# Moving a subtract from VectorE to GpSimd while a recurrence runs

## The chip, the cores and the metric

The kernel runs on one core of a Trainium2 chip. The metric is the device time of one execution in microseconds, the median of several runs. The engines of the core that matter here are TensorE (PE, matmuls), VectorE (DVE, elementwise work), ScalarE (ACT, activations and copies), GpSimd (POOL, here nearly idle) and the DMA queue that SyncE (SP) feeds.

## The reference

One layer of a decoder trunk, in float32, for a sequence of 1024 tokens and a width of 1024. Cut to what matters:

```python
h = rms_norm(x, norm_mix_pre)
proj = h @ w_in                                  # r, k, v, low ranks | S5 input | two gates
gates = jax.nn.sigmoid(proj[..., 2304:] + b_gate)
g_rwkv, g_s5 = jnp.split(gates, 2, axis=-1)
o_rwkv = rwkv7_branch(proj[..., :1792], ...) @ w_branch_rwkv     # a recurrence over the tokens
o_s5 = s5_branch(proj[..., 1792:2304], ...) @ w_branch_s5        # a diagonal state space model and a GLU (w_glu)
mixed = (g_rwkv * o_rwkv + g_s5 * o_s5) @ w_out
x = x + rms_norm(mixed, norm_mix_post)
h = rms_norm(x, norm_ffn_pre)
z = conv(h @ w_up)                               # causal, width 3
f = (gelu(gate) * val) @ w_down                  # gate, val: the halves of z
return x + rms_norm(f, norm_ffn_post)
```

The recurrence (RWKV-7) keeps a 64x64 state for each of 8 heads: `S = S * w + (S a) b' + v k'`, and each token reads `S r`.

## The kernel before, in words

**Matmuls in two parts.** Each operand of the large matmuls is split into a high part (rounded to the matmul's type, fp32r) and a low part (the float32 value less the high part). A product then takes three matmuls: high by high (L172), low activations by high weights (L173), high activations by low weights (L174). `mm3_steps` issues them for one 128x128 weight tile and 512 tokens; that is a step, and the kernel's planner counts 0.68 us for it.

**Weights.** `load_w` (L142) brings the weights in, 512 columns at a time: a DMA on SP's queue into a raw tile `wf` (L155), a cast by ScalarE into the high part `wh` (L156), and a subtract by VectorE into the low part `wl` (L157). There are 4 `wh` and 4 `wl` buffers; the raw tiles come from the pool `self.wp` (2 buffers) and, while `self.wfp` names a second pool, from that too (2 more). All of it is issued at the high priority HPW. L157 runs 171 times: for w_in, the low ranks, w_glu, w_br (the branch projections), w_out, and the first tiles of w_up.

**Stages.** `front_half` (L1816) runs the projections and the S5 branch, then, from L1850 on, the recurrence together with the rest of the mixing sub-layer. `build` goes on with the end of the mixing (`mix_out`), the up-projection (`fast_up`) and the down-projection (`down`).

**The recurrence.** The tokens come in two halves (th = 0, 1), each in 8 chunks of 64. For each half there is a preparation (`rwkv_front`), the inversion of triangular matrices (`rwkv_inv`: transposes at L784 and L798, then 30 pairs of short VectorE steps, L795 and L797, one after another, and copies at L773), a second level (`rwkv_level`: transposes at L812, matmuls at L822 and L832), the chain over 8 chunks (`rwkv_chain`: small matmuls, and U and S on VectorE at L890, L903, L904), and an output stage (`rwkv_out`). The matmuls of the projections, gates and merges are the filling between the small matmuls of these lanes.

**What sets the order.** The order on TensorE is written out by hand: `drive` (L185) takes a step of a lane when its due time has come by the planner's clock, and steps of the filling (`background`) otherwise. The order on the other engines is planned when the program is built, by priorities and estimated durations, and is fixed from then on; each engine works through its queue in order.

**The filling during the recurrence.** First the rest of the projections (r, k, v and gates, with their weights from w_in), then the merge of the first half of the tokens (`merge`): `gate` (L1198) multiplies a branch by its projection into a PSUM bank `gm` (2 banks in this stage) and VectorE empties the bank at L1203; `glu_tile` is the GLU of the S5 branch. Then follow the S5 branch's merge for the second half (`merge_s5`) and the output projection of the first half (`outproj(0, ...)`). When that is done `self.mark` is set and the stage ends (L1859).

**GpSimd's queue before.** In this stage it holds a few memsets (L624, L672), four small products (L627), the DMAs that export the bonus terms (L731, after VectorE's L730), and the DMAs that load late gates (L1195). At the very end of the kernel it does three adds (L1672).

Of the kernel before, what the change touches and what calls it, by code (L numbers as in the profile page):

```python
# [9 lines left out]
F32 = mybir.dt.float32  # L10
# [3 lines left out]
ALU = mybir.AluOpType  # L14
# [52 lines left out]
class Kern:  # L67
# [74 lines left out]
    def load_w(self, *srcs, pool=None):  # L142

        nc = self.nc
        wh, wl = [], []
        wp = pool or self.wp
        with self.tc.high_priority(HPW):
            for src in srcs:
                for o in range(0, src.shape[1], 512):
                    n = min(512, src.shape[1] - o)  # L150
                    h = wp.tile([128, 512], F32R, tag="wh", name=self.nm("wh"), bufs=4 if pool else NWH)
                    l = self.lx() if pool else wp.tile([128, 512], F32R, tag="wl", name=self.nm("wl"), bufs=NWL)
                    self.wfs = (self.wfs + 1) % (2 if self.wfp is None else 4)
                    f = (self.wp, self.wfp)[self.wfs // 2].tile([128, 512], F32, tag="wf", name=self.nm("wf"), bufs=NWF)
                    nc.sync.dma_start(f[:, :n], src[:, o:o + n])  # L155
                    nc.scalar.copy(h[:, :n], f[:, :n])  # L156
                    nc.vector.tensor_tensor(l[:, :n], f[:, :n], h[:, :n].bitcast(F32), ALU.subtract)  # L157
                    wh.append(h)
                    wl.append(l)
        return wh, wl  # L160
# [802 lines left out]
    def start(self, pool):  # L963
# [70 lines left out]
        for i in range(2):  # L1034
            for b in range(4):
                load_w(b, i)
            for k in range(4 * i, 4 * i + 4):
                if k:
                    load_x(0, k)
# [776 lines left out]
    def front_half(self):  # L1816

        tc = self.tc
        self.h = [None, None]
        self.now = self.credit = 0.0  # L1820
        self.wfs, self.wfp = 0, None
        self.fill_prio, self.acc = HPW, {}
        self.mark, self.chained = False, False
        self.s5_in_done, self.stored, self.mixed_in, self.all_in, self.open = -1, None, False, False, 0
        with tc.tile_pool(name="lxp", bufs=4) as self.lxp, tc.tile_pool(name="s5c", bufs=1) as self.s5c, \
                tc.tile_pool(name="u8p", bufs=1) as u8p, tc.tile_pool(name="eva", bufs=NEVA) as self.evp, \
                tc.tile_pool(name="psx", bufs=1, space=PSUM) as self.psx:
            self.ps, self.ngm = self.psx, 4
            self.u8 = [u8p.tile([128, 8, 128], F32, name=f"u8_{b}") for b in range(4)]
            with tc.tile_pool(name="xp", bufs=1) as xp:  # L1830
                with tc.high_priority(HPN):
                    self.setup(xp)
                    self.s5w = {}
                    self.start(xp)
                    self.setup_vecs()
                with tc.high_priority(HP):
                    self.s5_setup()
                self.fill = [self.mix_in()] + [self.gate_tiles(m) for m in range(14)] + [
                    self.merge_loads(), self.gate_tiles(14, 15)]
                self.outs, self.yr = 0, []  # L1840
            with tc.tile_pool(name="s5p", bufs=1) as self.s5p:
                self.s5d = [{} for _ in range(4)]
                self.tabs = self.s5_done = -1
                self.drive([(HP2, self.s5_lane()), (HP, self.tab_lane())])
                self.drain(lambda: self.mixed_in and not self.open)
        self.early_stack = ExitStack()
        self.rka = self.early_stack.enter_context(tc.tile_pool(name="rka", bufs=1, side="right"))
        with tc.tile_pool(name="evb", bufs=NEV) as self.evp, tc.tile_pool(name="rk", bufs=1) as self.rk, \
                tc.tile_pool(name="psy", bufs=1, space=PSUM) as self.psx:
            self.ps, self.ngm = self.psx, 2  # L1850
            self.rwkv_setup()
            self.wfp = self.rk
            self.ds = [[{}, {}], [{}, {}]]
            self.grams = 0
            self.fronts, self.masked, self.preps, self.chains, self.chunks, self.outs, self.z = 0, 0, 0, 0, 0, 0, {}
            self.pts = [self.tg("pt", 2, (128, 8, 4)) for th in range(2)]
            mg, self.mx0, self.first, self.ys5, self.xs5, self.brk, self.fac = [], [], [], [], [], [], []
            self.drive([(HP2, self.prep_lane(0)), (HP2, self.prep_lane(1)), (HP2, self.chain_lane()), (HP, self.out_lane(mg))])
            self.drain(lambda: self.mark)  # L1859
            self.wfp = None  # L1860

    def s5_lane(self):
        for b in range(4):
# [143 lines left out]
```

## Time and profile before

| | |
|---|---|
| median of 3 runs | 1463.06 us (1462.29 to 1465.25) |
| the profiled execution | 1461.26 us, its span 1459.5 us |
| granted TensorE clock, mean | 0.986 |
| busy: TensorE, VectorE, ScalarE, GpSimd | 1402.2, 1087.5, 746.7, 34.9 us |
| L157, all 171 | 117.2 us on VectorE, 688 ns each |
| L156, all 171 | 105.2 us on ScalarE, 618 ns each |

How to read the lines of a profile: a row of a group or of a timeline names the engine, the line of the kernel, the operation, the output and the inputs by the names of their tiles, the shape and type, and the count; in brackets or behind a bar stands the idle time of the engine just before, and what ended it (its releaser). L157 is line 157 of the kernel before. A row of a table by stretches gives for each stretch of the span the busy microseconds and, in brackets, the number of instructions of each engine, then the granted clock of TensorE (1.00 is full speed), the share of time that the DMA engines were busy, and GB/s. A row of waits reads: who waited, for whom, microseconds in total, how often, the longest.

### The profile page before, as it was taken

Reading aid. Unit: us, or ns where it says so; the run is one execution under the profiler, and the core shown is the slowest. Engines: PE = TensorE matmul, PEld = TensorE weight load, DVE = VectorE, ACT = ScalarE, POOL = GpSimd, SP = SyncE. Lnnn points to the kernel's source line nnn. Section 1 sums busy time; section 2 is a strip of 40 time slices with the busy share of each in tenths; the row PEclk is TensorE's granted clock in tenths of the full one; section 3 lists DMA queues with packets and bytes.
Section 4 is the critical chain, followed back from the end, with each engine's and each line's share of the span. In section 5 each row is a group of like instructions: output and inputs, shape, how many; then the busy total and the mean of one; then the engine's idle time right before and its main releaser. Section 6 shows DMA issues by size and latency. Waiting matters only on the chain. (4 is left out here: it accounts for less than half of the span.)

```text
span 1459.5 us, 23887 instructions
## 1 busy us (share of the span) xinstructions
PE 1402.2 (96%) x9156; PEld 1142.9 (78%) x9156; DVE 1087.5 (75%) x1783; ACT 746.7 (51%) x1197; POOL 34.9 (2%) x80
## 2 busy tenths in 40 slices
PE   7999999999999989899999999999999999999996
PEld 5778888878878767678788887888888887888785
DVE  8986886378327788548688898777777777597677
ACT  7667775453424564535455464454544445444451
POOL 0000000000000000000000000000000000000001
PEclk9999999999999999899999999999999999999998
DMA  7454433542413565433555543222222228934723
GB/s 221 116 190 128 144 117 108 188 146 80 139 60 110 162 193 165 138 111 116 172 195 180 158 133 122 87 83 76 75 84 87 87 73 273 328 112 144 239 79 115
DMA packets 119682, 202.04 MB, mean 138 GB/s; under 512 B 28672, under 2 KB 34944, under 8 KB 119568
## 3 DMA queue, kind: packets, MB, share of 16 engines
q1 hardware_dynamic: 113296, 182.43, 39.4%
q0 software_dynamic: 4544, 15.80, 2.9%
q10 hardware_dynamic: 1728, 2.29, 0.4%
q8 instruction: 72, 1.18, 0.3%
q14 instruction: 42, 0.34, 0.1%
HBM read 148.04 MB, written 50.33 MB: 136 GB/s over the span
## 5 line engine op out<-in xcount | busy, mean ns | idle before, releaser
L172 PE MATMUL gm<-hh,wh 128*128 128x512 f32 x672 | 276.2, 411 | 9.1 <-DVE hl L1203 4.6
L173 PE MATMUL gm<-hl,wh 128*128 128x512 f32 x672 | 264.8, 394 | 0.0
L174 PE MATMUL gm<-hh,wl 128*128 128x512 f32 x672 | 264.6, 394 | 0.0
L156 ACT CAST wh<-wf 128x512 fp32r<-128x512 f32 x171 | 105.2, 618 | 140.9 <-PE gm L173 72.5
L157 DVE TENSOR_TENSOR wl<-wf,wh 128x512 fp32r<-128x512 f32 x171 | 117.2, 688 | 76.2 <-ACT wh L156 75.6
L172 PEld LDWEIGHTS gm<-hh,wh 128*128 128x128 f32 x672 | 127.5, 190 | 41.5 <-DVE hl L1203 5.7
L174 PEld LDWEIGHTS gm<-hh,wl 128*128 128x128 f32 x672 | 127.7, 190 | 27.8
L173 PEld LDWEIGHTS gm<-hl,wh 128*128 128x128 f32 x672 | 127.8, 190 | 24.7 <-issue 1.0
L1626 PE MATMUL d<-xl,wh 128*128 128x512 f32 x308 | 120.7, 392 | 2.1 <-DVE xl L227 2.0
L1625 PE MATMUL d<-xh,wh 128*128 128x512 f32 x308 | 120.8, 392 | 2.1 <-ACT xh L226 2.1
L1627 PE MATMUL d<-xh,wl 128*128 128x512 f32 x308 | 120.6, 392 | 0.0
L1451 PE MATMUL rp<-t,h 128*128 128x512 f32 x216 | 84.4, 391 | 1.5 <-ACT p L1465 1.5
L1453 PE MATMUL rp<-t,l 128*128 128x512 f32 x216 | 84.2, 390 | 0.5 <-DVE l L227 0.5
L1452 PE MATMUL rp<-t,h 128*128 128x512 f32 x216 | 84.1, 389 | 0.0
L1626 PEld LDWEIGHTS d<-xl,wh 128*128 128x128 f32 x308 | 58.2, 189 | 15.5 <-DVE xl L227 3.4
L1625 PEld LDWEIGHTS d<-xh,wh 128*128 128x128 f32 x308 | 58.2, 189 | 14.6 <-ACT xh L226 2.4
L1627 PEld LDWEIGHTS d<-xh,wl 128*128 128x128 f32 x308 | 58.1, 189 | 12.0
L226 ACT CAST h<-r 128x1024 fp32r<-128x1024 f32 x34 | 35.8, 1054 | 61.1 <-PE rp L1452 29.6
L227 DVE TENSOR_TENSOR l<-r,h 128x1024 fp32r<-128x1024 f32 x34 | 41.6, 1225 | 29.2 <-ACT h L226 27.7
L1472 DVE SCALAR_TENSOR_TENSOR y<-zv,vecs,y 128x1023 f32<-128x1023 f32 (+1 forms) x36 | 46.1, 1281 | 8.5 <-ACT y L1470 8.5
L1465 ACT COPY p<-rp 128x512 f32<-128x512 f32 x54 | 31.0, 574 | 36.6 <-PE rp L1453 36.6
L1451 PEld LDWEIGHTS rp<-t,h 128*128 128x128 f32 x216 | 40.5, 188 | 11.1 <-ACT p L1465 2.4
(459 smaller groups left out, 3127.6 us busy)
## 6 DMA issues: line engine op xcount, KB each, us to landing
r<-in_w_up_dram SPq DMA_DIRECT2D x36, 512.0 KB, 3.6
wf<-in_w_in_dram SPq DMA_DIRECT2D x62, 256.0 KB, 3.0
st<-in_w_down_dram SPq DMA_DIRECT2D x55, 256.0 KB, 4.0
st<-ACT SPq DMA_DIRECT2D x44, 256.0 KB, 4.3
wf<-in_w_up_dram SPq DMA_DIRECT2D x36, 256.0 KB, 2.9
ACT<-y POOLq DMA_DIRECT2D x18, 512.0 KB, 2.9
GT<-ev SPq DMA_DIRECT2D x32, 256.0 KB, 2.5
wf<-in_w_br_dram SPq DMA_DIRECT2D x32, 256.0 KB, 2.6
```

Of the source, the lines that this page charges most:

```text
L156: nc.scalar.copy(h[:, :n], f[:, :n])
L157: nc.vector.tensor_tensor(l[:, :n], f[:, :n], h[:, :n].bitcast(F32), ALU.subtract)
L172: mm(ps, a, xh[k], start=k == 0, stop=False)
L173: mm(ps, a, xl[k], start=False, stop=False)
L174: mm(ps, b, xh[k], start=False, stop=k == n - 1)
L1451: mm(ps, wh[:, c], xh, start=first and k == 0, stop=False, skip_group_check=True)
L1452: mm(ps, wh[:, c], xl, start=False, stop=False, skip_group_check=True)
L1453: mm(ps, wl[:, c], xh, start=False, stop=k == 3, skip_group_check=True)
L1472: V.scalar_tensor_tensor(y[:, lag:], z[:, 0:1024 - lag], self.vec(nme, i), y[:, lag:], ALU.mult, ALU.add)
L1625: mm(ps, wh[:, c], xh[:, x], start=start, stop=False, skip_group_check=True)
L1626: mm(ps, wh[:, c], xl[:, x], start=False, stop=False, skip_group_check=True)
L1627: mm(ps, wl[:, c], xh[:, x], start=False, stop=stop, skip_group_check=True)
```

## The change

`load_w` takes the engine of the subtract from a new attribute, `self.weng`. It is VectorE at the start, GpSimd from the moment at which the recurrence's stage names its second pool for raw tiles, and VectorE again when that stage has ended. Nothing else is edited: the casts, the loads and TensorE's order stay as they are.

```diff
@@ load_w
                     nc.scalar.copy(h[:, :n], f[:, :n])
-                    nc.vector.tensor_tensor(l[:, :n], f[:, :n], h[:, :n].bitcast(F32), ALU.subtract)
+                    self.weng.tensor_tensor(l[:, :n], f[:, :n], h[:, :n].bitcast(F32), ALU.subtract)
@@ front_half, at its start
-        self.wfs, self.wfp = 0, None
+        self.wfs, self.wfp, self.weng = 0, None, self.nc.vector
@@ front_half, after rwkv_setup
-            self.wfp = self.rk
+            self.wfp, self.weng = self.rk, self.nc.gpsimd
@@ front_half, when the stage has ended
-            self.wfp = None
+            self.wfp, self.weng = None, self.nc.vector
```

In the program's order 33 of the 171 loads come before the switch, 78 while it is set (30 of w_in, 24 of w_br, 8 of w_glu, 16 of w_out), and 60 after it.

## The prediction

> **What bounds the kernel now.** I read the first two parts of the page first, then the table by stretches, then what TensorE waited for, and only then single rows.
>
> ```profile
> span 1459.5 us, 23887 instructions
> PE 1402.2 (96%) x9156; PEld 1142.9 (78%) x9156; DVE 1087.5 (75%) x1783; ACT 746.7 (51%) x1197; POOL 34.9 (2%) x80
> ```
>
> TensorE (PE) is busy for 96% of the span and GpSimd (POOL) for 2%. So a gain can only come out of the idle time of TensorE, or out of its clock, in the stage that the change touches. The table by stretches shows how much that is (columns: stretch, its length, busy us and count of PE, PEld, DVE, ACT, POOL, then granted clock, DMA share, GB/s; the sum runs over 250 to 712).
>
> ```profile
> 450.00:500.00 50.00, 47.69 (x350) 39.34 (x349) 44.43 (x90) 29.38 (x60) 1.08 (x2) 0.97 0.47 144
> 500.00:550.00 50.00, 43.53 (x297) 34.03 (x297) 41.00 (x85) 28.88 (x52) 1.08 (x2) 0.97 0.63 196
> 550.00:600.00 50.00, 41.13 (x325) 32.87 (x325) 42.26 (x80) 27.82 (x51) 0.00 (x0) 0.89 0.56 172
> 650.00:700.00 50.00, 50.00 (x410) 40.27 (x400) 37.73 (x75) 25.26 (x46) 2.13 (x4) 1.00 0.33 101
> sum 462.00, PE 440.03 PEld 350.11 DVE 296.13 ACT 219.54 POOL 8.80; mean PE 44.00 PEld 35.01 DVE 29.61 ACT 21.95 POOL 0.88
> ```
>
> Over the whole recurrence TensorE idles 462.0 - 440.0 = 22 us, and 15.3 us of that lie between 500 and 600 (6.5 + 8.9), where VectorE (DVE) is 82 to 85% busy. At 650 to 700 VectorE is 75% busy and TensorE loses nothing. The waits of TensorE in the same window name what came late:
>
> ```profile
> PE gm L172 <- DVE hl L1203: 4.6, 2, 3.9
> PE gm L172 <- DVE ev L1203: 3.1, 2, 2.2
> PE rp L822 <- DVE ld L812: 3.0, 1, 3.0
> PE cz L822 <- ACT hh L231: 2.2, 1, 2.2
> PE rp L756 <- DVE ld L730: 1.7, 1, 1.7
> ```
>
> No line names L157, the subtract that the change moves. TensorE waits for PSUM banks that the gating of the merges (L1203, on VectorE) has not yet emptied, and for small steps of the recurrence. So the subtract matters only as work that stands ahead of those steps in VectorE's queue.
>
> **The change part by part.** Which instructions move: the 33 loads before the switch keep VectorE, the 60 after it too, and 171 - 33 - 60 = 78 move. The windows of that line show them, the first row for the stretch of the second inversion, the second for all:
>
> ```profile
> L157 DVE TENSOR_TENSOR wl<-wf,wh x171: 644/689/737, 48.1 to 879.0; 128x512 fp32r<-128x512 f32 x171
> 523.00:569.00 46.00, 10.26 (x15) 0.96 0.58 182
> 273.00:700.00 427.00, 53.33 (x78) 0.98 0.42 134
> ```
>
> Removed from VectorE: 78 x 0.69 = 53.3 us of busy time. Added to POOL: the same instruction on GpSimd. The nearest rows are the three subtracts' cousins at the very end, of the same 128x512 size with two SBUF inputs, and the VectorE work beside them:
>
> ```profile
> L1672 POOL TENSOR_TENSOR r<-r,A x2: 1262/1472/1682, 1448.6 to 1449.9; 128x512 f32<-128x512 f32 x2
> L1672 DVE TENSOR_TENSOR r<-r,A x2: 679/699/719, 1449.7 to 1451.7; 128x512 f32<-128x512 f32 x2
> 1448.64 2.94 POOL L1672 TENSOR_TENSOR r<-r,A 128x512 f32<-128x512 f32 x2 [211.48 <-DVE r L1671]
> 1449.74 0.72 DVE L1672 TENSOR_TENSOR r<-r,A 128x512 f32<-128x512 f32 x1
> 1451.85 1.65 POOL L1672 TENSOR_TENSOR q<-q,A 128x512 f32<-128x512 f32 x1 [0.27 <-DVE q L1671]
> 1451.69 0.68 DVE L1672 TENSOR_TENSOR r<-r,A 128x512 f32<-128x512 f32 x1
> ```
>
> One takes 1.26 us, and 1.65 to 1.68 us where a VectorE add with two SBUF inputs had begun just before it. That is 98 to 131 us on an otherwise idle engine. These rows also show a conflict: both stretched POOL instructions overlap such a VectorE add and lose 0.4 us each; the one VectorE add that began before a POOL add ended (1449.74, while POOL's first ran to 1449.90) took 0.719 us instead of 0.679, so 0.04 us over at most 0.16 of overlap.
>
> *Latency of the weights.* A tile's low part is needed by the third matmul, L174. The rows give the tightest tile (the first that moves) and a usual one of the merges (cast, subtract, first use):
>
> ```profile
> 273.15 2.19 ACT L156 CAST wh<-wf 128x512 fp32r<-128x512 f32 x4 [4.06 <-POOL rkb L627]
> 275.20 0.39 PE L174 MATMUL gm<-hh,wl 128*128 128x512 f32 x1
> 275.42 0.39 PE L172 MATMUL gm<-hh,wh 128*128 128x512 f32 x1
> 557.92 0.62 ACT L156 CAST wh<-wf 128x512 fp32r<-128x512 f32 x1 [1.86 <-issue]
> 558.66 0.68 DVE L157 TENSOR_TENSOR wl<-wf,wh 128x512 fp32r<-128x512 f32 x1
> 566.54 0.39 PE L174 MATMUL gm<-hh,wl 128*128 128x512 f32 x1
> ```
>
> In the usual case the use comes 8.0 us after the cast's end, with four tile buffers ahead of TensorE; a subtract of 1.7 us that waits 1 us more hides there, and its price without that cover would be about 0.6 us a tile. The first tile has its cast done at 273.15 + 2.19/4 = 273.7 and its use at 275.20, 1.5 us: the POOL subtract ends between 273.8 + 1.26 = 275.06 (hidden) and 273.8 + 1.68 = 275.5 (0.3 us late). I take 0.2 us.
>
> *Queues.* A moved subtract waits on POOL for its cast; behind it stand the four kinds of POOL work of this stage: the exports at L731, the memsets at L672 and L624, and the late gate loads at L1195. They can come up to 1.7 us later, and the exports are read back microseconds later. The other way round, a subtract can stand behind an export that waits for VectorE:
>
> ```profile
> 523.93 0.54 POOL L731 DMA_DIRECT2D bv<-ld  x1 [41.44 <-DVE mt L797]
> SPq L155 <- DVE wl L157: 103.3, 42, 7.5
> ```
>
> That costs TensorE nothing until it exceeds some 6 us (8.0 less 1.7). On SP's queue the reload of a raw tile waits for the subtract (103.3 us over 42 waits before), so the loads behind it start up to about 1 us later; the same cover hides it. Both at 0.
>
> *VectorE in the second inversion, 523 to 569.* Here 15 subtracts go. Each frees its pitch, 0.61 us (545.65 - 545.04), and one left VectorE idle for 1.22 us at the queue's head, so VectorE is relieved of 15 x 0.61 + 1.22 = 10.4 us.
>
> ```profile
> 536.72 0.69 DVE L157 TENSOR_TENSOR wl<-wf,wh 128x512 fp32r<-128x512 f32 x1 [1.22 <-ACT wh L156]
> 545.04 0.68 DVE L157 TENSOR_TENSOR wl<-wf,wh 128x512 fp32r<-128x512 f32 x1
> 545.65 0.40 DVE L795 TENSOR_TENSOR tm<-mt 128x240 f32<-128x240 f32 x1
> L795 DVE TENSOR_TENSOR tm<-mt x60: 191/346/409, 338.6 to 565.4; 128x30 f32<-128x30 f32 x4, 128x58 f32<-128x58 f32 x4, 128x84 f32<-128x84 f32 x4, 128x108 f32<-128x108 f32 x4
> ```
>
> Against that stands the conflict. The inversion is a string of short steps with two SBUF inputs (L795 and L797, median 0.35 us each), so POOL gets its turn within a few tenths of a microsecond, and the next step then finds POOL reading. What a POOL subtract costs VectorE no row shows at length: the bounds are 0 (VectorE always goes ahead, as in the two overlaps where it began first) and the whole 1.26 us. I take 0.9 us, nearer the upper end, because the 0.04 us above is a hold and not a sharing of bandwidth, and because in this stretch VectorE is hardly ever without such a step. That makes 15 x 0.9 = 13.5 us, net 13.5 - 10.4 = +3.1 us on VectorE.
>
> Where does that reach TensorE? Not through the inversion's result: its last copies end at 570.3 and the transposes that read it start at 591.18. It reaches it through the queue's order, at this place:
>
> ```profile
> 565.89 2.23 DVE L798 STREAM_TRANSPOSE mt<-mt 128x1024 f32<-128x1024 f32 x1
> 568.02 0.64 DVE L157 TENSOR_TENSOR wl<-wf,wh 128x512 fp32r<-128x512 f32 x1
> 568.58 1.70 DVE L773 COPY gr<-mt 32x512 f32<-32x512 f32 x4
> 570.31 1.28 DVE L1203 SCALAR_TENSOR_TENSOR ev<-ev,gm 128x512 f32<-128x512 f32 x2
> 571.14 0.47 PE L172 MATMUL gm<-hh,wh 128*128 128x512 f32 x1 [2.17 <-DVE ev L1203]
> 572.03 0.63 PE L172 MATMUL gm<-hh,wh 128*128 128x512 f32 x1
> 591.18 1.43 DVE L812 STREAM_TRANSPOSE ld<-gr 32x512 f32<-32x512 f32 x2
> ```
>
> The gating at 570.31 stands behind the end of the inversion, and TensorE waits 2.17 us for it. If VectorE's order stays, this wait grows by the 3.1 us. The order is planned when the program is built, though, and with 15 subtracts out of it the inversion's steps move ahead of the gatings by up to 10.4 us of plan; then the hold of 13.5 us stands ahead of a gating, less the one PSUM bank that TensorE may run ahead (a gate tile is four steps of three matmuls at a pitch of 275.42 - 275.20 = 0.22 us, 2.7 us): 10.8 us. Between 3.1 and 10.8 I take 4.5, nearest to the order that the trace shows. Stalls also cost clock: after the 2.17 us a matmul takes 0.63 us at 572.03 instead of 0.39. The stretch from 550 to 600 has four of the waits above (2.2, 0.9, 3.0 and 2.2 us) and a granted clock of 0.89, which is 5.5 us lost in 50, 1.4 us a wait; I add one such loss. Elsewhere the relief and the hold about cancel, and TensorE has no wait there; for the shorter of the two waits on L1203 with `hl` (4.6 - 3.9 = 0.7 us), which has a subtract right ahead of the late gating, I give back 0.8 us with what lies around it.
>
> The sum: 0.2 + 4.5 + 1.4 - 0.8 = +5.3 us. The profiled execution took 1461.3 us (span 1459.5 and 1.8 around it), so 1466.6; the median of the runs is 1463.1, 1.8 above it, so 1468.4.
>
> A rule bears on the hold. The Trainium skill, "SBUF — State Buffer", section "Who interferes with whom", says that a VectorE instruction with two SBUF inputs contends with a GpSimd instruction that reads SBUF, and that whoever comes second is blocked until the first has finished. The trace agrees as far as it goes: POOL, second, lost 0.4 us, and VectorE, second, lost 0.04. By that rule each hold would be the full 1.26 us, and VectorE's net in the stretch 18.9 - 10.4 = +8.5 instead of +3.1 us.
>
> **The rivals.** *Full hold (heavier than my forecast).* Every POOL subtract stops VectorE for its whole 1.26 us: the wait at 571.14 grows by 8.5 us or, with the new order, by 18.9 - 2.7 = 16 us; with two clock losses 1463 + 11 to 19, 1474 to 1482. For it: the density of two-input steps, and the 0.04 us. This is also what the Trainium skill's section above would give. Against it: many casts fall where VectorE reads PSUM or transposes. Chance 0.15.
>
> *VectorE goes first (faster).* If POOL yields whenever VectorE has a step ready, the hold falls below the 0.61 us that a subtract frees, which is the point from which this decides. Then the 10.4 us of relief are real: the waits on L1203 of 0.7 and 2.2 us, 0.6 of the L812 wait and the 1.4 us of clock go, and some of L730's 1.7: about -5.5 us, 1457.5. For it: both clear overlaps in the trace were won by VectorE without loss. Against it: those two had begun first. Chance 0.26.
>
> *Nothing to see (within 0.2%).* The hold is about 0.6 us, equal to the pitch that is freed, or the gains and losses meet; 1463 give or take 2.9 us (0.2%, about what a measurement of this kernel can tell from no change). For it: TensorE waits on no subtract, and 400 of the 427 us have no wait that a subtract explains. Chance 0.27.
>
> *A blocked POOL queue.* An export that waits for VectorE (L731) is planned ahead of subtracts and comes more than 6 us later than they could have run; then TensorE waits for L157 itself, each microsecond beyond one to one, 1463 + 7 or so. The 41.44 us in the row above were an idle engine's wait, not a delay. Chance 0.02.
>
> **How the numbers follow.** My forecast, slower by about 5 us, gets 0.30. Slower by over 0.2% is that with the full hold and the blocked queue: 0.47. Within 0.2%: 0.27. Faster: 0.26. The range has to reach the faster case and most of the full hold: 1456 to 1479. For the likeliest case alone it is 1466 (the low end of 3.1 us) to 1474.
>
> **What would show it.** Right: 78 subtracts on POOL, at 1.3 to 1.9 us; VectorE steps with two SBUF inputs (L795, L797, L227, L232, L1249) longer by tenths in the mean, or standing with idle time that nothing explains; the wait of TensorE on L1203 above its 7.7 us; the clock of 550 to 600 not above 0.89. Wrong: L795 at its 346 ns median and maximum near 409 while POOL runs, with TensorE's idle time below 22 us (VectorE goes first), or TensorE waiting for POOL at L174 (a blocked queue, or 1.5 us too short for the first tile).

## The result, and the profile after

The changed kernel takes 1486.44 us (median of 6 runs, 1479.61 to 1490.36), the kernel before 1462.67 us in the same comparison: a ratio of 1.0162, 95% interval 1.0131 to 1.0194, so slower by 23.8 us. The profiled execution took 1488.83 us. One execution on record lies far off all others, 3588 us in the run with 41 moved subtracts below, and the ratio given there leaves it out.

The first two parts of the changed kernel's page:

```profile
span 1487.0 us, 23914 instructions
PE 1412.5 (95%) x9156; PEld 1149.1 (77%) x9156; DVE 1081.0 (73%) x1705; ACT 745.5 (50%) x1197; POOL 141.9 (10%) x158
```

78 instructions have left VectorE (1783 to 1705) and its busy time has hardly fallen: 1087.5 to 1081.0 us. TensorE is busy for 10.3 us longer, with the same 9156 matmuls. To see where, I mark three matmuls that are the same in both kernels, as TensorE's order is (its 9156 matmuls come from the same lines in the same order): one that ends a wait of 1.05 us just before the stage, the first of L701 for the second half of the tokens, and the first of the mixing's end. From the timelines, before and then after (start, duration, ..., idle before):

```profile
269.15 0.50 PE L172 MATMUL gm<-hh,wh 128*128 128x512 f32 x1 [1.05 <-ACT ev L1158]
495.21 0.66 PE L701 MATMUL rp<-csts,gr 128*128 128x128 f32 x4 [2.03 <-ACT ld L937]
709.92 0.50 PE L172 MATMUL mm<-e,wh 128*128 128x512 f32 x1 [0.97 <-ACT mx L1327]
```

```profile
269.76 0.50 PE L172 MATMUL gm<-hh,wh 128*128 128x512 f32 x1 [1.05 <-ACT ev L1158]
509.18 0.66 PE L701 MATMUL rp<-csts,gr 128*128 128x128 f32 x4 [1.70 <-ACT ld L937]
733.47 0.50 PE L172 MATMUL mm<-e,wh 128*128 128x512 f32 x1 [0.97 <-ACT mx L1327]
```

The stage took 440.77 us before and 463.71 after, +22.9. Its first part, up to L701, went from 226.06 to 239.42, +13.4; its second from 214.71 to 224.29, +9.6. The tables by stretches for the whole stage, before and after:

```profile
269.15:709.92 440.77, 419.85 (x4632) 333.12 (x4632) 289.78 (x568) 214.56 (x422) 8.80 (x25) 0.98 0.42 134
```

```profile
269.76:733.47 463.71, 426.43 (x4633) 336.49 (x4633) 283.43 (x490) 213.44 (x422) 115.82 (x103) 0.96 0.41 128
```

TensorE's idle time (length less busy) went from 20.9 to 37.3 us, +16.4; the other 6.6 us are matmuls that took longer, and the granted clock fell from 0.98 to 0.96. What TensorE waited for between 250 and 740, after:

```profile
PE gm L172 <- DVE hl L1203: 12.2, 4, 6.5
PE gm L172 <- ACT ev L1158: 8.8, 4, 6.3
PE cz L715 <- DVE bk L703: 2.6, 1, 2.6
PE gm L174 <- POOL wl L157: 0.8, 1, 0.8
```

Two of these were short before, in rows not shown yet:

```profile
PE gm L172 <- ACT ev L1158: 1.1, 1, 1.1
PE cz L715 <- DVE bk L703: 0.8, 1, 0.8
```

L1203 has grown from 7.7 us (both its rows) to 12.2, L1158 on ScalarE, a matter of 1.1 us before, to 8.8, and L703 from 0.8 to 2.6. For a subtract itself TensorE waited once, 0.8 us. Two groups show the moved work and what it does to a VectorE step (ns min/median/max):

```profile
L157 POOL TENSOR_TENSOR wl<-wf,wh x78: 1264/1291/2190, 274.7 to 723.6; 128x512 fp32r<-128x512 f32 x78
L795 DVE TENSOR_TENSOR tm<-mt x60: 202/360/1584, 341.9 to 575.5; 128x30 f32<-128x30 f32 x4, 128x58 f32<-128x58 f32 x4, 128x84 f32<-128x84 f32 x4, 128x108 f32<-128x108 f32 x4
```

The median of L795 hardly moves (346 to 360), the longest goes from 409 ns to 1584. One place of the timeline shows why:

```profile
546.58 0.36 DVE L795 TENSOR_TENSOR tm<-mt 128x198 f32<-128x198 f32 x1
546.79 1.26 POOL L157 TENSOR_TENSOR wl<-wf,wh 128x512 fp32r<-128x512 f32 x1 [5.27 <-ACT wh L156]
546.97 1.31 DVE L797 TENSOR_TENSOR mt<-mt,tm 128x198 f32<-128x198 f32 x1
```

Two steps of the same size: the first takes 0.36 us, the second, begun 0.18 us after the GpSimd subtract, takes 1.31, and ends 0.23 us behind it (548.28 against 548.05). VectorE does not count as idle there; it counts as busy with a longer step. This is why its busy time did not fall.

### The profile page after: what moved, and what is told of

Same layout as the page of the kernel before. It is cut to its first block, busy times and chain, and to the rows that moved or that the text cites. A ratio compares the mean times of both kernels' runs of the same rounds, so it can differ in the third digit from the quotient of the medians.

```text
span 1487.0 us, 23914 instructions
## 1 busy us (share of the span) xinstructions
PE 1412.5 (95%) x9156; PEld 1149.1 (77%) x9156; DVE 1081.0 (73%) x1705; ACT 745.5 (50%) x1197; POOL 141.9 (10%) x158
## 4 chain that ended last, share of the span: by engine, by line
PE 59%; DVE 8%; DMA 3%; ACT 2%; issue 1%; SPq 0%; ACTq 0%; DVEq 0%
PE d L1625 5%; PE d L1626 5%; PE d L1627 5%; PE rp L1451 4%; PE rp L1453 4%; PE rp L1452 4%; PE gm L172 4%; PE gm L173 3%; PE gm L174 3%; PE mm L1451 2%; PE mm L1453 2%; PE mm L1452 2%; PE ch L172 2%; PE ch L173 2%; PE mm L172 2%; PE mm L173 2%
## 5 line engine op out<-in xcount | busy, mean ns | idle before, releaser
L172 PE MATMUL gm<-hh,wh 128*128 128x512 f32 x672 | 278.1, 414 | 21.9 <-DVE hl L1203 12.2
L172 PEld LDWEIGHTS gm<-hh,wh 128*128 128x128 f32 x672 | 128.4, 191 | 57.4 <-DVE hl L1203 13.4
L157 POOL TENSOR_TENSOR wl<-wf,wh 128x512 fp32r<-128x512 f32 x78 | 105.2, 1352 | 309.5 <-ACT wh L156 288.6
L157 DVE TENSOR_TENSOR wl<-wf,wh 128x512 fp32r<-128x512 f32 x93 | 63.7, 687 | 27.5 <-ACT wh L156 26.8
L1465 ACT COPY p<-rp 128x512 f32<-128x512 f32 x54 | 31.0, 574 | 39.5 <-PE rp L1453 39.5
```

The costliest lines, as they stand in the source:

```text
L157: self.weng.tensor_tensor(l[:, :n], f[:, :n], h[:, :n].bitcast(F32), ALU.subtract)
L172: mm(ps, a, xh[k], start=k == 0, stop=False)
```

## The experiments

A second thing differs between the kernels. The order of the queues is planned when the program is built, and without the 78 subtracts the planner moved VectorE's inversion steps ahead of other work, and on ScalarE the copies of L773 ahead of evictions. So there are two suspects, the hold and the order, and three theories: the hold alone (theory 1), the order alone (theory 2), both together, an order planned for a relieved VectorE meeting one that is stopped (theory 3). To part them, the orders were written out and forced (an ordering edge from each instruction to the one wanted before it on its engine). TensorE's order is the same throughout.

**All 78 on GpSimd, order of before on VectorE, ScalarE and SyncE.**

```diff
+        pin(order of the kernel before: VectorE without the 78, ScalarE, SyncE)
```

> The 78 subtracts run on GpSimd, and VectorE, ScalarE and SyncE keep the order of the kernel before. Theory 1 (hold: each GpSimd subtract stops VectorE's two-input steps): the loss stays, 1480 to 1487 us. Theory 2 (the new order of the queues alone makes TensorE wait): the loss is gone, 1463 us or less. Theory 3 (both are needed, an order planned for a relieved VectorE met by a VectorE that is stopped): between, 1466 to 1476.

1472.74 us, ratio 1.0079 (1.0052 to 1.0107).

**The changed kernel's order, and GpSimd reads nothing.**

```diff
-   self.weng.tensor_tensor(l, f, h, ALU.subtract)       # where weng is GpSimd
+   nc.gpsimd.memset(l, 0.0)
+   pin(order of the changed kernel, on all four)
```

> The order of all queues is that of the changed kernel, but each of the 78 subtracts on GpSimd is a memset to zero: GpSimd reads nothing, and the low parts of these weights are left out. Theory 1 (hold): the loss is gone, 1455 to 1463 us. Theory 2 (order): the loss stays, 1480 us or more. Theory 3 (both needed): 1455 to 1466 us, with the wait of TensorE on L1158 near 373 us shrunk to under 2 us.

1464.75 us, ratio 0.9999 (0.9976 to 1.0022).

**The same memsets, order of before.**

```diff
-   self.weng.tensor_tensor(l, f, h, ALU.subtract)
+   nc.gpsimd.memset(l, 0.0)
+   pin(order of the kernel before)
```

> The 78 subtracts are memsets to zero on GpSimd (low parts left out), and the order of the queues is that of the kernel before: VectorE is relieved, nothing reads on GpSimd, nothing is reordered. All theories: 1463 us or less, 1452 to 1462; it is the ceiling of what the relief of VectorE can bring. If it is slower than 1466 us, something besides hold and order costs time (GpSimd's writes, or the later start of the reloads).

1458.69 us, ratio 0.9975 (0.9955 to 0.9996).

VectorE's totals on the pages of these three, in this order:

```profile
PE 1406.3 (96%) x9156; PEld 1146.6 (78%) x9156; DVE 1085.6 (74%) x1705; ACT 746.4 (51%) x1197; POOL 138.7 (9%) x158
```

```profile
PE 1405.8 (96%) x9156; PEld 1146.2 (78%) x9156; DVE 1043.4 (71%) x1705; ACT 746.3 (51%) x1197; POOL 75.7 (5%) x158
```

```profile
PE 1403.5 (96%) x9156; PEld 1145.2 (79%) x9156; DVE 1042.6 (72%) x1705; ACT 747.6 (51%) x1197; POOL 76.2 (5%) x158
```

The zeros show no effect on TensorE's rate over the stage: it is busy for 420.0 us in the last run, 419.85 before. A memset differs from the subtract in one more way: it waits for no cast and takes 0.53 us instead of 1.29, so the low part is ready sooner. TensorE's waits on L157 come to 0.8 us in the changed kernel, and no row of the run with the reads and the old order names it, so this can hardly be what parts the runs. The relief is 1087.5 - 1042.6 = 44.9 us of VectorE. With the reads on, at the same order, 1085.6 - 1042.6 = 43.0 us come back, 0.55 us for each subtract. What is left is 1.9 us. Theories 1 and 2 both fall (1472.7 is under 1480; 1464.8 is under 1480): each suspect alone, net of the relief, costs less than half of what both cost. Theory 3 holds, within its numbers for both times; the wait on L1158 in the run with memsets was 2.1 us where it said under 2. In ratios, reads cost 1.0% at the old order and 1.6% at the new one; the new order costs 0.2% without reads and 0.8% with them. That the two make each other worse rests on a difference of 0.6% whose own interval is about 0.5% (the four half-widths, 0.2 to 0.3%, taken together); in the stage lengths of the single profiled executions, below, they simply add.

**The hold by itself.** A separate kernel; VectorE and GpSimd have buffers of their own.

```python
dve_two:  V.tensor_tensor(o, a, b, ALU.add)        # a, b in SBUF     dve_psum: a in PSUM
dve_copy: V.tensor_copy(o, a)
pool_sub: G.tensor_tensor(g, c, d, ALU.subtract)   # 128x512          pool_set: G.memset(g, 1.0)
```

> A kernel of its own that computes nothing of the reference: VectorE adds of 128x512 with two SBUF inputs alone, GpSimd subtracts alone, then GpSimd subtracts beside VectorE adds of 128x512, beside VectorE adds of 128x128, beside VectorE adds with one PSUM input, beside VectorE copies, and GpSimd memsets beside VectorE adds. Theory 1 (hold): VectorE's two-input stretches last longer by 0.5 to 1.3 us for each GpSimd subtract, with a PSUM input and beside memsets by under 0.1 us. Theory 2: by under 0.1 us everywhere.

Its timeline, the phases one after another (L32 two SBUF inputs, L35 one in PSUM, L38 copy; L41 subtract, L44 memset):

```profile
9.85 4.90 DVE L32 TENSOR_TENSOR o<-ina,inb 128x512 f32<-128x512 f32 x8
15.60 7.36 POOL L41 TENSOR_TENSOR g<-inc,ind 128x512 f32<-128x512 f32 x6 [0.51 <-DVE ind L28]
23.59 16.11 DVE L32 TENSOR_TENSOR o<-ina,inb 128x512 f32<-128x512 f32 x16
23.75 9.98 POOL L41 TENSOR_TENSOR g<-inc,ind 128x512 f32<-128x512 f32 x6 [0.51 <-DVE ind L28]
40.41 16.18 DVE L32 TENSOR_TENSOR o<-ina,inb 128x128 f32<-128x128 f32 x48
57.34 9.66 DVE L35 TENSOR_TENSOR o<-z,inb 128x512 f32<-128x512 f32 x16
57.47 7.38 POOL L41 TENSOR_TENSOR g<-inc,ind 128x512 f32<-128x512 f32 x6 [0.51 <-DVE ind L28]
67.72 14.52 DVE L38 COPY o<-ina 128x512 f32<-128x512 f32 x24
67.88 8.38 POOL L41 TENSOR_TENSOR g<-inc,ind 128x512 f32<-128x512 f32 x6 [0.51 <-DVE ind L28]
82.96 9.72 DVE L32 TENSOR_TENSOR o<-ina,inb 128x512 f32<-128x512 f32 x16
```

Alone, 8 adds take 4.90 us (0.61 each), and 6 subtracts 7.36 (1.23 each). Beside 6 subtracts 16 adds take 16.11 us; beside memsets (last row) 9.72. That is 6.39 / 6 = 1.06 us of VectorE for each subtract, and GpSimd loses (9.98 - 7.36) / 6 = 0.44 us for each. With one input in PSUM neither engine loses anything (9.66, 7.38). VectorE's copies have a single SBUF input and are held all the same. Of their row of 24, the first seven (six of them beside a subtract, at 1.48 us) and the 16 behind the last subtract, by themselves:

```profile
L38 DVE COPY o<-ina x7: 420/1479/1486, 67.7 to 75.1; 128x512 f32<-128x512 f32 x7
76.80 5.45 DVE L38 COPY o<-ina 128x512 f32<-128x512 f32 x16
```

A copy alone takes 5.45 / 16 = 0.34 us, so 24 would take 8.2; they took 14.52, again 6.3 / 6 = 1.06 us for each subtract, and GpSimd loses (8.38 - 7.36) / 6 = 0.17 us. Theory 1's hold is there as told, 1.06 us within its 0.5 to 1.3; of copies it had said nothing. The Trainium skill, "SBUF — State Buffer", section "Who interferes with whom", says that a VectorE instruction with two SBUF inputs contends with a GpSimd instruction that reads SBUF, not with one that only writes it, and that one with at most one SBUF input doesn't contend outside VectorE's 2-port modes. The rows of the adds, of the PSUM input and of the memsets agree. The held copies are that exception, if they ran in such a mode; which mode they ran in no view here shows.

**What holds, and how finely.** The same, with GpSimd copies, with subtracts of 128x128, and with VectorE adds of 128x128 alone.

```diff
+pool_copy:  G.tensor_copy(g, c)                          # 128x512, one input
+pool_small: G.tensor_tensor(g, c, d, ALU.subtract)       # 128x128
```

> A kernel of its own that computes nothing of the reference: VectorE adds of 128x128 alone; GpSimd copies of 128x512 (one SBUF input) alone and beside VectorE's two-input adds; GpSimd subtracts of 128x128 alone and beside the adds; GpSimd subtracts of 128x512 beside VectorE steps of the form (a x 0.5) + b. If what holds VectorE is any GpSimd read of SBUF, a copy holds it as a subtract does, by about its own length. If it is the two inputs on GpSimd's side, VectorE isn't held by the copies. Small subtracts: the same hold per element, about 0.3 us for each 128x128.

```profile
9.71 4.93 DVE L32 TENSOR_TENSOR o<-ina,inb 128x128 f32<-128x128 f32 x24
15.40 3.39 POOL L49 COPY g<-inc 128x512 f32<-128x512 f32 x6 [0.42 <-DVE inc L28]
19.42 13.01 DVE L32 TENSOR_TENSOR o<-ina,inb 128x512 f32<-128x512 f32 x16
33.32 9.91 POOL L52 TENSOR_TENSOR g<-inc,ind 128x128 f32<-128x128 f32 x24 [0.51 <-DVE ind L28]
43.85 25.54 DVE L32 TENSOR_TENSOR o<-ina,inb 128x512 f32<-128x512 f32 x32
```

48 adds of 128x128 would take 2 x 4.93 = 9.9 us and took 16.18 beside 6 subtracts: 1.05 us a subtract again, so the size of the VectorE step doesn't matter. A GpSimd copy (0.57 us alone) holds the adds for (13.01 - 9.72) / 8 = 0.41 us, a 128x128 subtract (0.41 us alone) for (25.54 - 2 x 9.72) / 24 = 0.25 us. In all three cases the hold is GpSimd's own time less some 0.16 us. One input on GpSimd's side is enough. Steps of the form (a x 0.5) + b beside six subtracts took 16.10 us, like the adds.

**Which subtracts cost.** Order of before; 50 of the 78 on GpSimd, those of the two inversions on VectorE. (k counts the 78 in the program's order, from 0.)

```diff
-   self.weng.tensor_tensor(...)
+   (self.weng if not (9 <= k <= 13 or 30 <= k <= 52) else nc.vector).tensor_tensor(...)
```

> Order of the kernel before; 50 of the 78 subtracts run on GpSimd, and the 28 that fall into the two inversions and the microseconds behind them stay on VectorE. Theory A (the hold costs where the inversions' short two-input steps stand back to back): most of the 9.5 us of the run with all 78 and the old order are gone, 1462 to 1467 us. Theory B (the hold costs at the first step ahead of the inversions, the wait on L703 near 305 us, or evenly over the subtracts): 1468 to 1472 us.

1468.81 us, ratio 1.0041 (1.0024 to 1.0058). Then the 28 others alone:

```diff
+   (self.weng if 9 <= k <= 13 or 30 <= k <= 52 else nc.vector).tensor_tensor(...)
```

> The counterpart: order of the kernel before; only the 28 subtracts of the inversions run on GpSimd, the other 50 stay on VectorE. Theory A: 1467 to 1473 us. Theory B: 1463 to 1467 us. VectorE's extra time per subtract, against the run with memsets, near 1.0 us under both.

1470.41 us, ratio 1.0043 (1.0026 to 1.0060). VectorE's busy time on the page of the 28 is 1095.0 us; with 28/78 of the relief of 44.9 it would be some 1071.4, so by this estimate the reads put back 23.6 / 28 = 0.84 us for each, where near 1.0 was expected. The two parts add up to the whole (0.41 + 0.43% against 0.79%), and neither theory is right alone: the inversions cost about as much as the rest. The waits of TensorE with all 78 and the old order, between 250 and 740, name both places:

```profile
PE gm L172 <- DVE hl L1203: 8.2, 5, 5.3
PE cz L715 <- DVE bk L703: 3.9, 1, 3.9
```

The second row is the front of the first half near 300 us: a string of VectorE steps with two SBUF inputs (L693 to L695) ends at L703, and TensorE stands there for 3.9 us instead of 0.8. The reads are not the only thing that does this, though. With the memsets and the changed kernel's order, so without any read, the wait is there too:

```profile
PE cz L715 <- DVE bk L703: 3.3, 1, 3.3
```

With the memsets and the old order it is gone (under 0.1 us). So at this place the hold alone and the order alone cost some 3 us each, and the two together hardly more (2.6 us in the changed kernel, 4.1 in two later runs with its order there).

**Only where TensorE has no wait.** Order of before; the first 14 and those of the second inversion stay on VectorE.

```diff
+   (self.weng if 14 <= k <= 29 or 53 <= k else nc.vector).tensor_tensor(...)
```

> Order of the kernel before; only the 41 subtracts that lie where TensorE has no wait (between the inversions and behind the second) run on GpSimd, the first 14 and those of the second inversion stay on VectorE. If a hold costs nothing where TensorE doesn't wait for VectorE: no change, 1460 to 1465 us. If the hold costs everywhere in proportion: 41 of 78 of 9.5 us, 1467 to 1469.

1463.86 us, ratio 0.9997 (0.9981 to 1.0013): 41 subtracts on GpSimd, and no change. They do hold VectorE: its busy time on the pages fell from 1087.5 to 1080.5 us, by 7.0, where 41/78 of the relief would be 23.6. Where nothing of TensorE's waits for VectorE the hold is free, and the relief is worth nothing either. Of the 50 subtracts of the run above, then, it is the nine left over (k 0 to 8, between 273 and 323 us, six of them ahead of the wait on L703) that cost the 0.41%.

**One edit to the order.** The first inversion in the changed kernel: ScalarE, VectorE and TensorE.

```profile
356.82 0.68 ACT L1158 ACTIVATE ev<-gm,hb_b_gate 128x512 f32<-128x512 f32 x1
370.32 2.49 ACT L773 COPY gr<-mt 32x512 f32<-32x512 f32 x4 [12.81 <-DVE mt L798]
372.84 0.69 ACT L1158 ACTIVATE ev<-gm,hb_b_gate 128x512 f32<-128x512 f32 x1
368.28 2.01 DVE L798 STREAM_TRANSPOSE mt<-mt 128x1024 f32<-128x1024 f32 x1
373.58 0.80 PE L172 MATMUL gm<-hh,wh 128*128 128x512 f32 x1 [6.25 <-ACT ev L1158]
378.80 0.40 PE L172 MATMUL gm<-hh,wh 128*128 128x512 f32 x1
```

ScalarE stands for 12.81 us at the copies, which wait for the end of the inversion; the eviction that TensorE needs is queued behind them. In the kernel before an eviction stood ahead of them:

```profile
358.79 0.69 ACT L1158 ACTIVATE ev<-gm,hb_b_gate 128x512 f32<-128x512 f32 x1 [4.51 <-issue]
364.80 0.62 ACT L773 COPY gr<-mt 32x512 f32<-32x512 f32 x1 [5.32 <-DVE mt L798]
```

```diff
 ScalarE:  L1158, L156, L156, L1158,
-          L773 x4, L1158, L156, L156, L1158
+          L1158, L156, L156, L1158, L773 x4
```

> The changed kernel with its own order on every engine but one edit on ScalarE: in the first inversion the two evictions of L1158 and two casts go ahead of the four copies of L773, which wait for VectorE's L798. If the stall of 6.25 us near 384 us is the hold meeting that order, TensorE's wait there falls under 1 us and the time by 6 to 10 us (the stall and the slow clock behind it): 1476 to 1480. If the stall only moves on to the next wait, 1484 to 1488.

1479.53 us, ratio 1.0109 (1.0089 to 1.0129): 6.9 us of the 23.8 gone, and with it the stall (at 373.58; the 384 of the expectation is a slip). What is left on L1158:

```profile
PE gm L172 <- ACT ev L1158: 2.3, 3, 1.1
```

With the same order and no reads (the second run) this stall was 2.1 us. With the reads and the old order there was one of 2.2 us, 24 matmuls later. So the order alone and the hold alone cost some 2 us each here, and together 6.25, more than their sum. That fits the four subtracts in this inversion at 1.05 each behind an order without slack (2.1 + 4.2 = 6.3, an estimate from these rows).

**The order by halves.** All 78 on GpSimd; old order up to the second inversion, new from there, and the reverse.

```diff
+   pin(before[:start of the 2nd inversion] + after[start of the 2nd inversion:])
```

> All 78 subtracts on GpSimd; the order of the kernel before up to the second inversion, and from its first step on the order of the changed kernel on VectorE and ScalarE (the inversion's steps L795 and L797 ahead of gatings). With the old order throughout it was 1472.7 us, with the new one 1486.4. If the second inversion's order costs what remains beside the edit on ScalarE in the first (7 us), 1477 to 1481 us, with TensorE's two waits on L1203 of 2 to 3 us back. If the first part holds the whole cost of the order, 1471 to 1475.

1481.79 us, ratio 1.0123 (1.0100 to 1.0146), 0.8 above the expected 1477 to 1481. The waits on L1203 of 1.6 and 2.3 us are back.

```diff
+   pin(after[:start of the 2nd inversion] + before[start of the 2nd inversion:])
```

> The counterpart: all 78 on GpSimd; the new order up to the second inversion, the old one from there. With the stall of 6.25 us on L1158 back: 1477 to 1483 us. If the second inversion's order holds the whole cost: 1471 to 1475.

1486.52 us, ratio 1.0163 (1.0139 to 1.0186). The stall of 6.25 us is back, but the time is 3.5 us above the expected 1477 to 1483.

Both halves of the order cost something. By the medians they don't add: the new first half alone is already as slow as the whole change. The profiled executions, cut at the marks shown above, say where (length less that of the kernel before, us):

| | to L701 | from L701 | stage | TensorE idle |
|---|---|---|---|---|
| no reads, old order | +3.9 | -7.2 | -3.3 | 17.5 |
| no reads, new order | +6.9 | -1.0 | +5.9 | 23.2 |
| reads, old order | +8.5 | +5.9 | +14.4 | 29.0 |
| reads, old then new | +5.0 | +10.9 | +15.9 | 31.5 |
| reads, new then old | +16.9 | +5.2 | +22.1 | 37.5 |
| reads, new, eviction first | +6.9 | +9.2 | +16.1 | 32.6 |
| the changed kernel | +13.4 | +9.6 | +22.9 | 37.3 |

Of the +3.9 in the first row 3.0 are matmuls that took longer, not waits (TensorE is busy for 225.2 us there, 222.2 before). Each row is one execution, good to a few microseconds (rows with the same order in a part differ by up to 3.5). In the second part, with reads, the old order costs 5 to 6 us and the new one 9 to 11. In the first the old one costs 5 to 9, the new one 13 to 17, and 7 with the one edit. Why the median of "new then old" isn't some 4 us below the changed kernel stays open. VectorE's new order with ScalarE's old one in the same half was not run, so what each of these two orders costs by itself isn't shown.

No version here that does the whole arithmetic beats the kernel before. The memsets in the old order do, by 0.25%, and leave out the low parts; that is the most that freeing VectorE in this stage can bring at that order.

## Why the prediction was wrong

The forecast was 1468.4 us, range 1456 to 1479; the time is 1486.4. The side was right (slower), and so was the kind of mechanism, a hold that outweighs the relief and reaches TensorE through the order of the queues. But it was reckoned for one place of the stage only, and there at a wait that did not grow. The loss is 23.8 us where 5.3 were forecast. By the prediction's own steps:

- *The hold.* Taken as 0.9 us, with 1.26 the full one; measured by itself 1.05 to 1.06. Over 15 subtracts that is some 2 us. The row that I read as "0.04 us over at most 0.16 of overlap" was no evidence of a light hold: a hold is GpSimd's time less about 0.16 us, so in an overlap of 0.16 there is none to see. The 0.4 us that GpSimd lost there is the 0.44 us measured above.
- *The relief in the second inversion.* Taken as 10.4 us. The stretch from its first L795 to its L798, before, then with reads and with memsets at the same order:

```profile
522.77:565.89 43.12, 37.57 (x162) 30.23 (x163) 39.54 (x99) 24.18 (x47) 1.08 (x2) 0.96 0.59 184
```

```profile
529.78:578.89 49.11, 40.31 (x167) 31.37 (x166) 46.26 (x85) 25.00 (x48) 19.43 (x16) 0.93 0.51 157
```

```profile
524.17:564.23 40.06, 36.20 (x157) 29.58 (x158) 32.03 (x85) 25.08 (x47) 7.93 (x15) 0.96 0.60 187
```

  43.1 us before, 49.1 with reads, 40.1 without: the relief was 3.1 us, the hold 9.1 (13.5 predicted), the net +6.0 instead of +3.1. The busy time tells why both are smaller than reckoned. Without the subtracts VectorE is busy for 7.5 us less (39.5 to 32.0), but idle for 8.0 us instead of 3.6: it now waits once for TensorE (1.49 us at 538.38) and four times for ScalarE's L1187 (0.7 to 1.2 us). With the reads it is busy for 14.2 us more, 0.95 for each of the 15, and part of that only fills those gaps.
- *The second inversion and the queue's order.* The sum gave the stage's second part 4.5 + 1.4 - 0.8 = 5.1 us (the 0.8 given back belong to the wait of 0.72 us at 546.70). From L701 on the stage lost 9.6 us. That lies inside the bounds drawn, but partly by luck, because the wait that was to grow, 2.17 us behind the end of the inversion, did not. The same matmul waits 2.3 us with the reads and the old order, and not at all in the changed kernel. What grew are the waits on the gatings *inside* the inversion, where its steps had moved ahead, as the upper bound supposed: 3.9 to 6.5 us, 0.7 to 2.1, and a new one of 2.9.
- *"Elsewhere the relief and the hold about cancel, and TensorE has no wait there."* This is the step that failed. For VectorE's total the first half is right: 44.9 us of relief, 43.0 of hold. But it isn't the total that TensorE waits for. The stage's first part, which the sum gave 0.2 us, lost 13.4. At L703, the end of the front's steps, TensorE did have a wait before, 0.8 us, and so no slack; it became 2.6. In the first inversion I looked at VectorE's order alone and not at what ScalarE's would put behind the inversion's end: a stall of 6.25 us where there had been none. These two are 8.0 of the 13.4 us; 3.1 are matmuls that took longer (225.3 us against 222.2), and most of the rest are three waits of 0.8 to 1.6 us.
- *The clock.* One loss of 1.4 us; TensorE's busy time in the stage grew by 6.6. After the wait of 6.25 us a matmul took 0.80 us, and it was back at 0.40 only 5 us later.
- *The latency of the weights, GpSimd's queue, SyncE's reloads*: right in the main. The first tile, priced at 0.2 us, shows no wait; one of 0.8 us on L157 came at 406.38 instead. The run with 41 subtracts moved shows no cost at all.
- *The rivals.* The full hold came nearest (1474 to 1482), with a hold only 0.2 us too long; it too was reckoned for one inversion only. "VectorE goes first" is refuted by the small kernels. "Nothing to see" is what the 41 subtracts show, and is refuted for those that TensorE's waits depend on.

## What to carry to other kernels

Before work is moved to GpSimd beside a busy VectorE, count VectorE's instructions with two SBUF inputs in that stretch, and its float32 copies from SBUF to SBUF: where such steps stand back to back, each GpSimd instruction that reads SBUF costs them its own length less about 0.16 us, which here was more than the instruction had cost VectorE (1.05 against 0.61). Read busy time with care, since a held step counts as busy. And where the order is planned from estimated durations, taking work off one engine reorders the others too: compare the queues of every engine, and ask what now stands in line behind an instruction that waits.

## What the runs showed of the hardware that was not expected

VectorE and GpSimd take strict turns: with both queues full of such instructions, one add and one subtract follow each other at 9.98 / 6 = 1.66 us a pair, and neither side gets ahead. The loss follows the same rule on both sides, the other's step less some 0.16 us: VectorE loses 1.06 us to a subtract of 1.23, GpSimd 0.44 to an add of 0.61 and 0.17 to a copy of 0.34. A GpSimd copy with a single input holds VectorE as well (0.41 us), and VectorE's float32 copies, with a single input too, are held like the adds (1.06 us a subtract), while memsets and VectorE steps with one input in PSUM don't meet at all.
